# Transposing only the four quarters of a layer's normed rows, and forming the three sums of them afterwards

## The chip, the cores and the metric

The kernel runs on one core of one Trainium2 chip. The metric is the device time of one execution in microseconds (us). Before the change the median of three runs is 982.19 us (982.18 to 983.54). The core has a matrix engine (PE, with its weight loads PEld), a vector engine (DVE), a scalar engine (ACT), GpSimd (POOL) and the queue of SyncE (SP), which only starts transfers here. Each engine works through its own instructions in the order in which they were written; engines meet at semaphores.

## The reference, cut to what matters

```python
def reference(x, mem, norm_g, ...):
    for i in range(2):
        h = rmsnorm(x, norm_g[i])              # (512, 1024)
        mem_h = rmsnorm(mem, mem_norm_g[i])
        proj = jnp.einsum('bsd,de->bse', h, w_in[i])
...
        # layer 0: dilated-window attention, layer 1: grouped-query attention
        o_mem = memory_attention(q_mem, mem_h, ...)
        y = jnp.concatenate([o_mix, o_mem], axis=-1) * jax.nn.silu(gate)
        x = x + jnp.einsum('bse,ed->bsd', y, w_out[i])
    return x
```

The change concerns the step between `h = rmsnorm(...)` and the einsum with the input weights, once in each of the two layers.

## The kernel before, in words

**Products by Strassen's scheme.** The product of the normed rows `h` (512 tokens by 1024 features) with a block of weights is not made as eight products of quarters but as seven, in Winograd's form. For this `h` is cut into quarters: 11 and 12 are the feature halves of the first 256 tokens, 21 and 22 those of the other 256. Seven left operands are needed: 12, 11, S1 = 21 - 22, S2 = S1 - 11, S4 = 12 + S2, S3 = 11 - 21, and 22. They are used in this order (`PRODUCTS`, L350), and a product starts only when its operand is there.

**Two-part numbers.** Each operand goes into the PE as a high and a low part: ACT casts it (the high part, L157), DVE subtracts the high part from it (the low part, L160); both are in the helper `split`. The three matmuls of L163 to L165 make one product of two such pairs. The weights go the same way: a tile `wl` of 128x1024 comes by DMA, ACT casts it to `wh` (L285), DVE subtracts to get `wo` (L295). Sums of weight quarters are made by DVE (L251, L259) at the start and later by accumulating DMAs on the POOL queue. Below, "a weight's low part" is one instruction of L295.

**From rows to operands.** The rows lie with tokens on the partitions, in four blocks of 128 tokens (`xb[0..3]` in layer 0, `x1`, tiles `acc`, in layer 1). A PE matmul needs the features on the partitions, so every operand must be transposed. `norm_1` gets the sums of squares (ACT L451) and POOL the inverse root; `norm_2` scales the rows in place (DVE L458). `turn4` makes four 128x128 transposes on PE (L464) of one 128x512 piece into one PSUM bank `xT`, and `split` takes it out. `put_h` does that for one operand and one token block c. `sum_h` and `sums_h` make the three sums and S1 from the untransposed rows (DVE L499, L507 to L509), and `rest_h` then transposes S2, S4, S3 and 22. So there are 7 operands x 2 blocks x 4 = 56 transposes in a layer, in 14 groups.

**What sets the order.** Nothing is scheduled by a compiler: the Python code is the order on each engine. After each group of matmuls a `Driver` (one "slot") lets waiting generators take one step: those that take products out of PSUM, the weight stream (`W.advance`), and `prep` (layer 0) or `ev_o` (layer 1), which make the operands. The waits between engines are put in by the layer below, which also keeps two engines from using one PSUM bank at a time.

**Layer 0's start** is bare: x and the first weights arrive, and `norm`, transposes, splits and the weight sums follow each other with little else to do. The first product chunk is `s_chunk(512, H, ev_v0, pre=second)`; `second` puts the operands 12 and 11, `prep` the others. **Layer 1's operands** are made in `ev_o` under the end of layer 0's output projection and under `mem_kv(1, ...)`, the projection of the memory rows (matmuls with `act`, heads' transposes `qT`).

Of the kernel before, what the change touches and what calls it, by code (L numbers as in the profile page):

```python
# [11 lines left out]
F32R = mybir.dt.float32r  # L12
AF = mybir.ActivationFunctionType
ALU = mybir.AluOpType
# [12 lines left out]
MEM_STEP = 1, 1  # L27
MEM_D = 4
PD, W_EARLY = 1, True
EO = 1, 2, 1, 1, 1  # L30
YB = {"m": (2, 2), "k": (1, 1, 1), 0: (1, 2, 1), 1: (1, 2, 1)}
Y = [3, 2, 2, 2, 3, 2, 2, 1, 1, 1]

# [91 lines left out]
def trunk_kernel(ctx: ExitStack, tc: tile.TileContext, x, mem, wall, norm_g, mem_norm_g, gcol,  # L125
                 qn_a, kn_a, qn_b, kn_b, ident_d, mask_d, tab_a, tab_b, out):
    nc = tc.nc
    V, A, G, T = nc.vector, nc.scalar, nc.gpsimd, nc.tensor
# [8 lines left out]
    def big(dt=F32, name="big"):  # L137
        return pool.tile([128, 2048], dt, tag="big", name=name, bufs=NBIG)

    def m4(dt=F32, name="m4"):  # L140
        return pool.tile([128, 1024], dt, tag="m4", name=name, bufs=NM4)

    def s2(dt=F32, name="s2"):
        return pool.tile([128, 512], dt, tag="s2", name=name, bufs=NS2)
# [4 lines left out]
    def at(name="at"):  # L149
        return psum.tile([128, 512], F32, tag="at", name=name, bufs=4)  # L150
# [4 lines left out]
    def split(hi, lo, src, act=True):  # L155
        if act:
            A.copy(hi, src)  # L157
        else:
            V.tensor_copy(hi, src)
        V.tensor_tensor(lo, src, hi.bitcast(F32), ALU.subtract)  # L160
# [282 lines left out]
    def norm_1(xb, both=False):  # L443

        ss = sm(2, "ss")
        for j in range(2):
            jk = s2(name="sq")
            if both and j:
                V.tensor_tensor_reduce(jk, xb[j], xb[j], 1.0 / 1024.0, 0.0, ALU.mult, ALU.add, ss[:, j:j + 1])
            else:  # L450
                A.activation(jk, xb[j], AF.Square, scale=1.0 / 32.0, accum_out=ss[:, j:j + 1])  # L451
        r, e = sm(1, "rstd"), sm(1, "mse")
        G.tensor_tensor(e, ss[:, 0:1], ss[:, 1:2], ALU.add)
        return rstd_of(e, 1)

    def norm_2(xb, r, row, js=(0, 1)):
        for j in js:
            V.scalar_tensor_tensor(xb[j], xb[j], r, row[j], ALU.mult, ALU.mult)  # L458

    def turn4(src, hi, lo, mid=None):  # L460

        p = at("xT")
        for k in range(4):
            T.transpose(p[:, k * 128:(k + 1) * 128], src[:, k * 128:(k + 1) * 128], ident)  # L464
        if mid:
            mid()
        split(hi, lo, p.rearrange("p (k t) -> p k t", k=4))

    def norm_3(xb, dst, c0, j):
        cs = slice(c0, c0 + 128)  # L470
        turn4(xb[j], dst.block(0, j, cs), dst.block(1, j, cs))
# [11 lines left out]
                mm3(p, sels[b](act, 0, kk), sels[b](act, 1, kk), w[k][0], w[k][1], kk == 0, kk == 7)  # L483
        chunk(2, len(sels), group, evac)

    part = {}

    def put_h(H, k, c, src, mid=None, early=False):

        if c == 0:  # L490
            part[k] = big(F32R, "h" + k).rearrange("p (a k t) -> p a k t", a=2, k=4)
        if c or early:
            H[k] = part[k]
        cs = slice(c * 128, (c + 1) * 128)
        turn4(src, part[k][:, 0, :, cs], part[k][:, 1, :, cs], mid)

    def sum_h(low):
        s1 = s2(name="xs1")
        V.tensor_tensor(s1, low[0], low[1], ALU.subtract)  # L499
        return s1  # L500

    def sums_h(H, top, low, c, s1, sums):

        (a11, a12), a21 = top, low[0]
        s2_, s4 = s2(name="xs2"), s2(name="xs4")
        put_h(H, "S1", c, s1)
        V.tensor_tensor(s2_, s1, a11, ALU.subtract)  # L507
        V.tensor_tensor(a21, a11, a21, ALU.subtract)
        V.tensor_tensor(s4, a12, s2_, ALU.add)  # L509
        sums.append((s2_, s4, a21, low[1]))  # L510

    def rest_h(H, sums, d=1):
        for i, k in enumerate(("S2", "S4", "S3", "22")):
            for c in range(2):
                put_h(H, k, c, sums[c][i])
            yield d

    def head_sq(p, n=4):
        ss = sm(n, "hss")
# [21 lines left out]
    def halves(t):  # L541
        return [t[:, 0:512], t[:, 512:1024]]
# [7 lines left out]
    def row_bank(name, times=1):  # L550

        r = [at("row") for _ in range(2)]
        for j in (1, 0):
            for _ in range(times):
                T.matmul(r[j], ones, rows[name][j][0:1, :], start=True, stop=True)
        return r
# [282 lines left out]
    H, H2 = {}, {}  # L839
    xb = [halves(t) for t in xt]  # L840
    nst = {}

    def prep():

        s1, sums = [], []
        for c in range(2):
            norm_2(xb[2 + c], nst[2 + c], first)
            s1.append(sum_h(xb[2 + c]))
            yield 1
        for c in range(2):  # L850
            sums_h(H, xb[c], xb[2 + c], c, s1[c], sums)
            yield 1
        yield from rest_h(H, sums)

    def setup():

# [11 lines left out]
    first = row_bank("x0", WARM)  # L868
# [10 lines left out]
    def mid():  # L879
        busy(128)  # L880
        W.lo()
        nst[1] = norm_1(xb[1], BOTH)

    put_h(H, "12", 0, xb[0][1], mid, True)
    if W_EARLY:
        W.hi(True)
# [4 lines left out]
    def second():  # L891
# [9 lines left out]
        nst[3] = norm_1(xb[3], BOTH)  # L901

    drv.spawn(prep(), PD)
    drv.spawn(setup(), SET_AT)

# [264 lines left out]
    x1d = dram.tile([4, 128, D], F32, name="x1d", bufs=1)  # L1170
    row_load("x1", norm_g[1:2, :])

    x1b, sums_b = {}, []

    def ev_o(n, b, x1):
        if n:
            for j in range(2):
                nc.sync.dma_start(x1d[b][:, j * 512:(j + 1) * 512], x1[j])
            r = norm_1(x1)
            yield EO[0]  # L1180
            norm_2(x1, r, rows["x1"])
            x1b[b] = x1
            yield EO[1]
            if b < 2:
                put_h(H2, "12", b, x1[1])
                put_h(H2, "11", b, x1[0])
            else:
                s1 = sum_h(x1)
                yield EO[2]
                sums_h(H2, x1b[b - 2], x1, b - 2, s1, sums_b)  # L1190
            if b == 3:
                yield EO[3]
                yield from rest_h(H2, sums_b, EO[4])

    drv.spawn(mem_norm(1), MEM_B)
    out_proj(YW, ys, xv, ev_o, lambda: [m4(name="acc") for _ in range(2)])


# [302 lines left out]
```

## Time and profile before

| | |
|---|---|
| median of three runs | 982.19 us |
| the profiled execution: time, span | 981.91 us, 980.1 us |
| busy on POOL | 332.2 us (34%) |
| transposes of L464 in the trace | 48 of sums (`xs`), 64 of rows (`x`, `acc`), 32 of memory rows (`m`) |
| moved by DMA | 205.08 MB, mean 209 GB/s |

The span is the time from the first to the last instruction; it lies 1.8 us under the profiled execution's own time. PE does the matmuls and the transposes. A row of the chain of waits names, in order of time, the work that the end hung on, with its start, its length as the chain counts it (up to where the next piece could begin) and its line. A row of the timeline has the start, the busy time, engine, line and operation of one run of equal instructions. A row of the waits has who waited, for whom, how long in total, how often, and the longest.

### The profile page before, as it was taken

The page shows a single profiled execution, that of the slowest core. Times are in us where ns is not written, and L with a number is a line of the kernel's source. Part 1 is how long each engine was busy: PE and PEld are TensorE (multiplying, and loading weights), DVE is VectorE, ACT ScalarE, POOL GpSimd, SP SyncE. Part 2 cuts the span into 40 slices and gives each one's busy share as a digit, 9 for nine tenths or more (in the row PEclk, how much of TensorE's full clock was granted, in tenths as well). Part 3 has the DMA queues.
Part 4 walks back from the last instruction along what each step waited for, and adds up shares of the span by engine and source line. Part 5 has one row for each costly group of instructions (what it writes and reads, how often), then busy time and mean ns, then how long its engine had stood idle before and what let it go on. Part 6 is the DMA issues. An engine that isn't in the chain of part 4 may idle for free.

```text
span 980.1 us, 16658 instructions
## 1 busy us (share of the span) xinstructions
PE 953.1 (97%) x5728; PEld 839.5 (86%) x5728; DVE 825.1 (84%) x1489; ACT 645.7 (66%) x1623; POOL 332.2 (34%) x468
## 2 busy tenths in 40 slices
PE   8899999999999999999999989998999999998998
PEld 5789888888888888888899977887999999997786
DVE  6997788878888888888888998968789998889974
ACT  5556678686767676768676656455677766667650
POOL 1121424556555555555544010124533331011000
PEclk9999999999999999999999999999999999999999
DMA  8979846969686868686949795669695786786432
GB/s 328 329 267 322 227 97 183 290 129 266 152 253 154 251 157 248 158 249 136 271 124 295 228 251 158 258 224 329 168 209 140 189 220 165 230 207 148 144 129 86
DMA packets 86678, 205.08 MB, mean 209 GB/s; under 512 B 25025, under 2 KB 35777, under 8 KB 86594
## 3 DMA queue, kind: packets, MB, share of 16 engines
q1 hardware_dynamic: 70034, 146.28, 42.7%
q0 software_dynamic: 15264, 55.58, 30.1%
q10 hardware_dynamic: 1296, 2.16, 0.6%
q8 instruction: 45, 0.74, 0.3%
q14 instruction: 39, 0.32, 0.1%
HBM read 157.79 MB, written 12.65 MB: 174 GB/s over the span
## 4 chain that ended last, share of the span: by engine, by line
PE 75%; DVE 16%; DMA 3%; issue 2%; ACT 2%; POOL 1%; SPq 0%; DVEq 0%; POOLq 0%
PE pj L163 20%; PE pj L165 19%; PE pj L164 19%; DVE wo L295 4%; PE qT L534 2%; PE oo L1131 1%; PE sa L1029 1%; PE pt L1110 1%; PE sa L1025 1%; PE xT L464 1%; DMA od<-o 1%; DVE sn L370 1%; PE ptb L1333 1%; DVE nmb L1314 1%; DVE yS L763 1%
## 5 line engine op out<-in xcount | busy, mean ns | idle before, releaser
L295 DVE TENSOR_TENSOR wo<-wl,wh 128x1024 fp32r<-128x1024 f32 x255 | 315.5, 1242 | 8.4 <-ACT wh L285 8.0
L285 ACT CAST wh<-wl 128x1024 fp32r<-128x1024 f32 x255 | 269.9, 1059 | 74.1 <-PE pj L165 39.8
L163 PE MATMUL pj<-wh,hS 128*128 128x512 f32 (+1 forms) x448 | 164.3, 367 | 0.2 <-ACT sn L360 0.2
L164 PE MATMUL pj<-wo,hS 128*128 128x512 f32 (+1 forms) x448 | 158.1, 353 | 2.6 <-DVE wo L295 2.6
L165 PE MATMUL pj<-wh,hS 128*128 128x512 f32 (+1 forms) x448 | 158.1, 353 | 0.0
L163 PE MATMUL pj<-wh,h 128*128 128x512 f32 (+1 forms) x336 | 123.2, 367 | 0.0
L164 PE MATMUL pj<-wo,h 128*128 128x512 f32 (+1 forms) x336 | 118.8, 353 | 1.9 <-DVE wo L295 1.9
L165 PE MATMUL pj<-wh,h 128*128 128x512 f32 (+1 forms) x336 | 118.9, 354 | 0.0
L413 POOL TENSOR_TENSOR rstd<-mse,half 128x4 f32<-128x4 f32 (+2 forms) x98 | 103.4, 1055 | 8.2
L164 PEld LDWEIGHTS pj<-wo,hS 128*128 128x128 f32 x448 | 85.0, 190 | 13.4 <-DVE wo L295 3.5
L165 PEld LDWEIGHTS pj<-wh,hS 128*128 128x128 f32 x448 | 84.7, 189 | 12.4 <-DVE hS L160 0.3
L163 PEld LDWEIGHTS pj<-wh,hS 128*128 128x128 f32 x448 | 84.8, 189 | 10.3 <-ACT sn L360 0.4
L360 ACT COPY sn<-pj 128x512 f32<-128x512 f32 x132 | 73.6, 591 | 17.5 <-PE pj L165 17.1
L412 POOL TENSOR_SCALAR mse<-hss 128x4 f32<-128x4 f32 (+1 forms) x86 | 45.7, 532 | 110.2 <-ACT junk L522 103.2
L522 ACT ACTIVATE junk<-sn 128x128 f32<-128x128 f32 x264 | 79.0, 308 | 0.2 <-DVE sn L364 0.2
L973 POOL TENSOR_TENSOR ta<-sn,tabs 128x128 f32<-128x128 f32 (+1 forms) x64 | 37.0, 580 | 120.7 <-DVE sn L527 81.6
L164 PEld LDWEIGHTS pj<-wo,h 128*128 128x128 f32 x336 | 64.0, 191 | 9.5 <-DVE wo L295 2.2
L165 PEld LDWEIGHTS pj<-wh,h 128*128 128x128 f32 x336 | 63.7, 190 | 9.2 <-DVE h L160 0.2
L370 DVE TENSOR_TENSOR sn<-pj,sn 128x512 f32<-128x512 f32 x99 | 67.5, 683 | 4.6 <-PE pj L165 4.4
L163 PEld LDWEIGHTS pj<-wh,h 128*128 128x128 f32 x336 | 63.9, 190 | 7.3 <-ACT h L157 0.2
L269 POOL DMA_DIRECT2D wl<-wl x33 | 29.3, 887 | 114.5 <-DVE wo L295 70.1
L163 PE MATMUL pj<-hS,wh 128*128 128x256 f32 x192 | 55.9, 291 | 0.0
(229 smaller groups left out, 2455.7 us busy)
## 6 DMA issues: line engine op xcount, KB each, us to landing
wl<-in_wall_dram SPq DMA_DIRECT2D x222, 512.0 KB, 6.9
wl<-wl POOLq DMA_DIRECT2D x64, 512.0 KB, 5.8
wl<-in_wall_dram POOLq DMA_DIRECT2D x42, 512.0 KB, 8.3
od<-o SPq DMA_DIRECT2D x12, 256.0 KB, 5.2
og<-od SPq DMA_DIRECT2D x12, 256.0 KB, 5.9
odb<-o SPq DMA_DIRECT2D x12, 256.0 KB, 3.5
og<-odb SPq DMA_DIRECT2D x12, 256.0 KB, 4.6
x<-in_x_dram SPq DMA_DIRECT2D x4, 512.0 KB, 5.7
```

The source lines that it names most:

```text
L163: T.matmul(o, lh, rh, start=start, stop=False, skip_group_check=True)
L164: T.matmul(o, lh, rl, start=False, stop=False, skip_group_check=True)
L165: T.matmul(o, ll, rh, start=False, stop=stop, skip_group_check=True)
L269: G.dma_start(self.tile[key], self.tile[c, "T2", x], accum_op=ALU.add)
L285: A.copy(wh, self.tile[self.items[i]])
L295: V.tensor_tensor(wo, self.tile[key], wh.bitcast(F32), ALU.subtract)
L360: A.copy(t, b)
L370: V.tensor_tensor(t, b, t, ALU.subtract if q == "12" else ALU.add)
L412: G.tensor_scalar(e, ss, EPS, None, ALU.add)
L413: G.tensor_tensor(r, e, half[:, 0:n], ALU.pow)
L522: A.activation(jk, p[:, j * 128:(j + 1) * 128], AF.Square, scale=QS, accum_out=ss[:, j:j + 1])
L973: G.tensor_tensor(ta[:, 0:n], xn[:, 0:n, 0:32], ropeA[:, 0, b, s0:s0 + n], ALU.mult)
```

## The change

Only the four quarters are transposed. `put_h` (used for 12 and 11) also copies the whole transposed piece out of PSUM with ACT into a kept tile `f12` or `f11` of 128x1024. `diffs_h` transposes 22 and 21 of a block, copies 22 into `f22` with ACT, lets DVE form S1 and S3 out of PSUM (21) and the kept tiles, and splits S1. `rest_h` forms S2 and S4 on whole 128x1024 tiles in SBUF and splits S2, S4, S3 and 22 from there, each by one ACT cast and one DVE subtraction of 128x1024. Layer 1's `ev_o` takes one slot less before the S1 of a block.

```diff
-EO = 1, 2, 1, 1, 1
+EO = 1, 2, 1, 1
...
-    def turn4(src, hi, lo, mid=None):
+    def turn(src):
         p = at("xT")
         for k in range(4):
             T.transpose(p[:, k * 128:(k + 1) * 128], src[:, k * 128:(k + 1) * 128], ident)
+        return p.rearrange("p (k t) -> p k t", k=4)
+
+    def turn4(src, hi, lo, mid=None):
+        p = turn(src)
         if mid:
             mid()
-        split(hi, lo, p.rearrange("p (k t) -> p k t", k=4))
+        split(hi, lo, p)
+        return p
...
+    def whole(k, c):
+        if c == 0:
+            full[k] = m4(name="f" + k).rearrange("p (k t) -> p k t", k=4)
+        return full[k][:, :, c * 128:(c + 1) * 128]
+
+    def put_h(H, k, c, src, mid=None, early=False):
+        p = turn4(src, *slot(H, k, c, early), mid)
+        A.copy(whole(k, c), p)
+
+    def diffs_h(H, low, c):
+        f22 = whole("22", c)
+        A.copy(f22, turn(low[1]))
+        p = turn(low[0])
+        s1, s3 = whole("S1", c), whole("S3", c)
+        V.tensor_tensor(s1, p, f22, ALU.subtract)
+        V.tensor_tensor(s3, full["11"][:, :, c * 128:(c + 1) * 128], p, ALU.subtract)
+        split(*slot(H, "S1", c), s1)
+
-    def rest_h(H, sums, d=1):
-        for i, k in enumerate(("S2", "S4", "S3", "22")):
-            for c in range(2):
-                put_h(H, k, c, sums[c][i])
-            yield d
+    def rest_h(H, d=1):
+        def put(k, f):
+            H[k] = big(F32R, "h" + k).rearrange("p (a k t) -> p a k t", a=2, k=4)
+            split(H[k][:, 0], H[k][:, 1], f)
+        s2_, s4 = full["11"], full["12"]
+        V.tensor_tensor(s2_, full["S1"], s2_, ALU.subtract)
+        put("S2", s2_)
+        yield d
+        V.tensor_tensor(s4, s4, s2_, ALU.add)
+        put("S4", s4)
+        yield d
+        put("S3", full["S3"])
+        yield d
+        put("22", full["22"])
+        yield d
...
     def prep():
         for c in range(2):
-            norm_2(xb[2 + c], nst[2 + c], first)
-            s1.append(sum_h(xb[2 + c]))
+            norm_2(xb[2 + c], nst[2 + c], first, (1, 0))
             yield 1
         for c in range(2):
-            sums_h(H, xb[c], xb[2 + c], c, s1[c], sums)
+            diffs_h(H, xb[2 + c], c)
             yield 1
-        yield from rest_h(H, sums)
+        yield from rest_h(H)
...
             else:
-                s1 = sum_h(x1)
+                diffs_h(H2, x1, b - 2)
+            if b == 3:
                 yield EO[2]
-                sums_h(H2, x1b[b - 2], x1, b - 2, s1, sums_b)
-            if b == 3:
-                yield EO[3]
-                yield from rest_h(H2, sums_b, EO[4])
+                yield from rest_h(H2, EO[3])
```

**ACT in layer 0's start.** These are ACT's rows from the second block's operand 12 to the cast of the third weight tile. In square brackets stand the semaphores that an instruction waits for; `xT` is a PSUM bank of transposes, `wl_91` the third weight tile. Before:

```order
L157 CAST h12_134<-xT_172 128x4x128 [waits PE_49]
L157 CAST h11_179<-xT_180 128x4x128 [waits PE_49]
L451 ACTIVATE sq_188,ss_187<-x_80 128x512 [waits DMAHW7_49]
L451 ACTIVATE sq_190,ss_187<-x_80 128x512
L157 CAST h11_179<-xT_200 128x4x128 [waits PE_49]
L285 CAST wh_207<-wl_91 128x1024 [waits DMAHW6_49]
```

and now:

```order
L157 CAST h12_134<-xT_174 128x4x128 [waits PE_49]
L512 COPY f12_157<-xT_174 128x4x128 [waits DVE_49]
L157 CAST h11_182<-xT_183 128x4x128 [waits PE_49]
L512 COPY f11_190<-xT_183 128x4x128 [waits DVE_49]
L451 ACTIVATE sq_193,ss_192<-x_80 128x512 [waits DMAHW7_49]
L451 ACTIVATE sq_195,ss_192<-x_80 128x512
L157 CAST h11_182<-xT_205 128x4x128 [waits PE_49]
L512 COPY f11_190<-xT_205 128x4x128 [waits DVE_49]
L285 CAST wh_213<-wl_91 128x1024 [waits DMAHW6_49]
```

Three copies came between, and each waits for DVE: by its semaphore count, for the subtraction L160 that reads the same bank.

**DVE in layer 0's start.** These are DVE's rows around the operand S2; `wl_101` and `wl_103` are the weight tiles of the products S2. Before:

```order
L160 TENSOR_TENSOR hS2_346<-xT_347,hS2_346 128x4x128 [waits Activation_49]
L160 TENSOR_TENSOR hS2_346<-xT_354,hS2_346 128x4x128 [waits Activation_49]
L370 TENSOR_TENSOR sn_275<-pj_260,sn_275 128x512
L295 TENSOR_TENSOR wo_344<-wl_101,wh_343 128x1024
L160 TENSOR_TENSOR hS4_388<-xT_389,hS4_388 128x4x128 [waits Activation_49]
```

and now:

```order
L530 TENSOR_TENSOR f11_190<-fS1_298,f11_190 128x1024 [waits DVE_49]
L160 TENSOR_TENSOR hS2_358<-f11_190,hS2_358 128x1024 [waits Activation_49]
L370 TENSOR_TENSOR sn_277<-pj_262,sn_277 128x512
L295 TENSOR_TENSOR wo_355<-wl_101,wh_354 128x1024
L533 TENSOR_TENSOR f12_157<-f12_157,f11_190 128x1024
L160 TENSOR_TENSOR hS4_389<-f12_157,hS4_389 128x1024 [waits Activation_49]
L295 TENSOR_TENSOR wo_383<-wl_103,wh_382 128x1024
```

The sum stands right ahead of the subtraction that waits for ACT's cast of that sum, and the weights' low parts stand behind it.

**ACT before layer 1.** These are ACT's rows from the first normed block of layer 1 to the casts of two weight tiles of the memory projection. Before:

```order
L157 CAST h12_7877<-xT_7878 128x4x128 [waits PE_49]
L157 CAST h11_7885<-xT_7886 128x4x128 [waits PE_49]
L451 ACTIVATE sq_7898,ss_7897<-acc_7326 128x512
L451 ACTIVATE sq_7900,ss_7897<-acc_7326 128x512 [waits DVE_49]
L157 CAST h12_7877<-xT_7928 128x4x128 [waits PE_49]
L157 CAST h11_7885<-xT_7935 128x4x128 [waits PE_49]
L285 CAST wh_7956<-wl_7831 128x1024 [waits DMAHW7_49,PE_49,Activation_49]
```

and now:

```order
L512 COPY f12_7850<-xT_7843 128x4x128 [waits DVE_49]
L157 CAST h11_7852<-xT_7853 128x4x128 [waits PE_49]
L512 COPY f11_7860<-xT_7853 128x4x128 [waits DVE_49]
L451 ACTIVATE sq_7867,ss_7866<-acc_7291 128x512
L451 ACTIVATE sq_7869,ss_7866<-acc_7291 128x512
L157 CAST h12_7842<-xT_7897 128x4x128 [waits PE_49]
L512 COPY f12_7850<-xT_7897 128x4x128 [waits DVE_49]
L157 CAST h11_7852<-xT_7905 128x4x128 [waits PE_49]
L512 COPY f11_7860<-xT_7905 128x4x128 [waits DVE_49]
L285 CAST wh_7927<-wl_7796 128x1024 [waits DMAHW7_49,PE_49,Activation_49]
L285 CAST wh_7930<-wl_7798 128x1024 [waits DMAHW0_49,PE_49,Activation_49]
L517 COPY f22_7933<-xT_7934 128x4x128 [waits PE_49]
```

Four copies that wait for DVE stand ahead of the two weight casts, and the copy of 22, which DVE's first difference needs, stands behind the casts.

More of the change, by code (lines that the diff above doesn't have):

```diff
@@ L484, in proj_t, with slot @@
         chunk(2, len(sels), group, evac)
-    part = {}
-    def put_h(H, k, c, src, mid=None, early=False):
+    part, full = {}, {}
+    def slot(H, k, c, early=False):
         if c == 0:
@@ L494, in put_h @@
         cs = slice(c * 128, (c + 1) * 128)
[L495 to L510, printed above, removed]
-    def rest_h(H, sums, d=1):
-        for i, k in enumerate(("S2", "S4", "S3", "22")):
-            for c in range(2):
-                put_h(H, k, c, sums[c][i])
-            yield d
+        return part[k][:, 0, :, cs], part[k][:, 1, :, cs]
+    def whole(k, c):
[28 more added lines that the diff above has]
+        yield d
     def head_sq(p, n=4):
@@ L843, in prep @@
     def prep():
-        s1, sums = [], []
         for c in range(2):
-            norm_2(xb[2 + c], nst[2 + c], first)
-            s1.append(sum_h(xb[2 + c]))
+            norm_2(xb[2 + c], nst[2 + c], first, (1, 0))
             yield 1
         for c in range(2):
-            sums_h(H, xb[c], xb[2 + c], c, s1[c], sums)
+            diffs_h(H, xb[2 + c], c)
             yield 1
-        yield from rest_h(H, sums)
+        yield from rest_h(H)
     def setup():
@@ L1171, in trunk_kernel @@
     row_load("x1", norm_g[1:2, :])
-    x1b, sums_b = {}, []
     def ev_o(n, b, x1):
@@ L1181, in ev_o @@
             norm_2(x1, r, rows["x1"])
-            x1b[b] = x1
             yield EO[1]
```

## The prediction

> **What bounds the kernel now.** First the page: busy shares and the engines of the chain of waits.
>
> ```profile
> PE 953.1 (97%) x5728; PEld 839.5 (86%) x5728; DVE 825.1 (84%) x1489; ACT 645.7 (66%) x1623; POOL 332.2 (34%) x468
> PE 75%; DVE 16%; DMA 3%; issue 2%; ACT 2%; POOL 1%; SPq 0%; DVEq 0%; POOLq 0%
> ```
>
> Over the whole span PE is the bound, so transposes taken off PE look like pure gain. But the change touches two short stretches only, and a share over the span says nothing of them. So next the windows (length; then busy us of PE, PEld, DVE, ACT, POOL; granted clock, DMA share, GB/s) and the waits of these stretches.
>
> ```profile
> 20.00:40.00 20.00, 15.53 (x77) 11.92 (x76) 19.96 (x27) 9.66 (x14) 3.72 (x4) 1.00 0.98 293
> 40.00:60.00 20.00, 20.00 (x106) 16.93 (x105) 16.71 (x22) 14.04 (x27) 2.25 (x6) 1.00 0.66 239
> 665.00:675.00 10.00, 6.67 (x30) 5.30 (x30) 9.09 (x15) 4.89 (x13) 8.46 (x6) 0.86 1.03 354
> PE pj L164 <- DVE wo L295: 4.5, 4, 1.9
> PE xT L464 <- DVE xs L499: 3.3, 2, 1.9
> ```
>
> From 20 to 40 us DVE is busy without a gap and PE only 15.5 of 20 us: in layer 0's start DVE is the bound, and PE waits 4.5 us for weights' low parts. From 40 us on PE is full. Before layer 1 PE stands twice (3.3 us together) for the first difference `xs` (L499), which the change removes. The chain of waits in order of time shows layer 0's start:
>
> ```profile
> 13.53 1.07 ACT h L157 x2
> 14.60 1.23 ACT sq L451 x4
> 15.83 0.48 ACT h L157
> 16.31 0.95 ACT wh L285
> ...
> 18.43 1.41 DVE x L458 x2
> ...
> 26.00 0.60 DVE hS L160
> ...
> 37.74 1.14 DVE wo L295
> ...
> 38.93 0.50 PE pj L164
> ...
> 45.34 0.87 PE xT L464 x8
> 46.21 0.23 PE pj L163
> ```
>
> The end hangs on ACT from 13.5 to 17.3, then on DVE to 38.9, and only then on PE, which issues one 128x512 matmul each 0.23 us. Between 13.5 and 39 us no transpose lies on it. These rows also give the step of each kind, the time until the next can begin: ACT 0.48 for 512 columns, 0.95 for 1024 and 1.23 for a block's squares, DVE 0.60, 1.14, and 0.70 for half a block's norm, a pair of groups of transposes 0.87.
>
> **Layer 0, ACT's part.** The change adds an ACT copy behind each split of 12 and 11, out of the bank that DVE's subtraction L160 reads. By the order with its waits the copy waits for that subtraction. Does such a wait cost? The nearest row is another pair of readers of one bank:
>
> ```profile
> DVE ks L985 <- ACT ks L984: 25.4, 16, 2.3
> L157 ACT CAST h<-xT x12: 583/590/594, 9.1 to 689.7; 128x512 fp32r<-128x512 f32 x12
> L160 DVE TENSOR_TENSOR h<-xT,h x12: 680/684/692, 9.7 to 690.5; 128x512 fp32r<-128x512 f32 x12
> 13.53 1.07 ACT L157 CAST h<-xT 128x512 fp32r<-128x512 f32 x2 [2.92 <-PE xT L464]
> 14.15 1.29 DVE L160 TENSOR_TENSOR h<-xT,h 128x512 fp32r<-128x512 f32 x2 [1.76 <-ACT h L157]
> 17.29 1.23 DVE L295 TENSOR_TENSOR wo<-wl,wh 128x1024 fp32r<-128x1024 f32 x1
> ```
>
> L984 and L985 read different columns of one bank and write different halves of `ks`, and DVE still waits 16 times for ACT (25.4 us). So the wait is real, if that row is read rightly. The Trainium skill ("PSUM — Partial Sum Buffer", section "PSUM bank collisions raise a hardware error") says that ScalarE and VectorE may not use one bank and quadrant at once, two reads included, and that one must guard by bank; this speaks against a second reader, and the row agrees. Without that rule the three copies below would cost 3 x 0.48 = 1.4 us and no waiting.
>
> The price: cast 0.59, hand-over 0.03 (cast at 13.53, subtraction at 14.15), subtraction 0.68, hand-over 0.03, so the copy starts 1.33 us after its cast, and the next ACT instruction 0.48 later. Before, it came 0.48 after the cast. Each `put_h` so holds ACT 1.33 us longer. Of four, the first falls into the 2.92 us for which ACT stood idle before 13.53. The other three, the squares of the third block between them, stand ahead of the cast of the third weight tile. Its low part, which was DVE's at 17.29, comes at 17.29 + 3 x 1.33 = 21.3: **+4.0**. Bounds: +1.4 if the copies waited for nothing, +4.0 if all wait; I take 4.0, since the order holds the waits.
>
> **Layer 0, DVE's part.** From that low part to the one of the first S2 product DVE had no gap. It begins with the last row above; the next rows are its end, the low parts behind it, and the cost of a cast:
>
> ```profile
> L285 ACT CAST wh<-wl 128x1024 fp32r<-128x1024 f32 x255 | 269.9, 1059 | 74.1 <-PE pj L165 39.8
> 37.67 1.21 DVE L295 TENSOR_TENSOR wo<-wl,wh 128x1024 fp32r<-128x1024 f32 x1
> 40.00 2.35 DVE L295 TENSOR_TENSOR wo<-wl,wh 128x1024 fp32r<-128x1024 f32 x2
> ```
>
> In this stretch of 20.38 us the change takes out eight sums (8 x 0.60) and two subtractions for S2 (1.20), 6.0 us. It puts in four differences (2.40), the whole S2 and its subtraction (2.28), a wait of 0.1 for the first cast of S1 and one of about 1.2 for ACT's cast of S2: 1.06 us (L285 has this shape) and hand-overs, with DVE standing, since nothing lies between the sum and its subtraction. Together 6.0: a draw. The other S1 waits are covered by the difference S3 (0.60). So the first S2 weight is ready at 41.8 + 1.2 = 43.0 instead of 38.9, +4.1.
>
> For the second S2 product the low part came at 40.00, 2.33 after the first. Now the sum S4, a wait of 1.2 and the subtraction stand ahead: 1.14 + 1.14 + 1.2 + 1.14 = 4.6, so it starts at 46.4 and ends at 47.6. PE, done with the first at 45.5, stands 2.1 us for it, then needs 11 more steps of 0.23 and is through at 50.1. Before, PE went on to S4 at 46.0 (46.21 as the chain counts), after the transposes at 45.34. From there the casts of S3 and 22 wait for no new sum, DVE leads again (S3's first low part is the sixth step of 1.14 from 46.4, near 53; PE needs it two products' halves of 12 steps after 50.1, at 55.6), and PE is the bound. **Layer 0: 50.1 - 46.0 = +4.1.** The transposes removed are in this (one pair, 0.87, lay at 45.34 where PE is the bound; the earlier ones lay in PE's waits). The delay lasts: PE is full afterwards.
>
> **Layer 1.** The rows (timeline, and PE's around the operands):
>
> ```profile
> 656.13 1.07 ACT L157 CAST h<-xT 128x512 fp32r<-128x512 f32 x2
> 661.04 1.05 ACT L285 CAST wh<-wl 128x1024 fp32r<-128x1024 f32 x1 [0.78 <-ACT h L157]
> 663.10 1.28 DVE L160 TENSOR_TENSOR h<-xT,h 128x512 fp32r<-128x512 f32 x2
> 665.22 4.27 POOL L413 TENSOR_TENSOR rstd<-mse,half 128x4 f32<-128x4 f32 x1
> 672.33 1.09 PE L534 MATMUL qT<-ident,xn 128*128 128x128 f32 x4
> 677.05 1.03 PE L464 MATMUL xT<-ident,xs 128*128 128x128 f32 x8
> ...
> 688.60 1.04 PE L464 MATMUL xT<-ident,acc 128*128 128x128 f32 x8
> 689.39 0.36 PE L163 MATMUL pj<-wh,hS 128*128 128x256 f32 x1
> ```
>
> ACT: two `put_h` from 656.13 on are done 2 x 1.81 later, 659.7, and the squares (1.23) at 661.0, where the next block's cast stands. Its subtraction stands on DVE behind two weights' low parts (663.10); only then come the copy (663.8), cast, subtraction and copy of 11 (to 666.1), and the two weight casts, at 666.1 instead of 661.0. The copy of 22 comes behind them, at 668.0 to 668.6. DVE, done with the last block's norm at 666.9 (two steps of 0.70 from 665.5, the end of the last L160 of 12 and 11), waits for it. Then L520, L521 and the subtraction (1.9), two low parts (2.3), the second block's three (1.9) and the heads' multiply (0.6): 675.4. PE has only the last block's transposes (0.87 from 666.9) and twelve matmuls of 0.23 until 670.5, and then waits for that: `qT` starts at 675.45 instead of 672.33, +3.1. The removed waits for `xs` are replaced by a longer one.
>
> Against this, PE's work from `qT` to the first S1 product took 689.39 - 672.33 = 17.1 us, with four pairs of transposes that are gone (the first and the last are quoted; 4 x 0.87 = 3.5): by PE S1 could start at 689.0, -0.4. But DVE must have its weight's low part: from 675.4 the sum S2 1.1, cast (behind two weight casts on ACT) 1.5, subtraction 1.1, heads 0.6, two low parts 2.3, a block of memory keys 0.7 (put at a norm's step), S4 with its cast 3.4, keys again 0.7, then S3's subtraction, whose cast stands on ACT behind two weight casts (from 685.4: three casts, 3.0), at 688.4 to 689.5, and the low part, 690.7. S1's second matmul (the first to read it) was at 689.6. **Layer 1: +1.1.** The lower bound is -3.5, the transposes alone, if `qT` kept its place and DVE kept up; the upper +3, if POOL's inverse root for the heads takes 4.27 us again and holds the multiply.
>
> **Edits costed at nothing.** The 128x1024 tiles `f` take five buffers of the pool that the weights use, but the row tiles `x` and `acc` go free earlier; in the start the weight loads behind them move by about the same 4 us. If a load came late, it would cost one load less its lead. The added ACT work later in layer 0 (S2's to 22's casts, four of 0.95 instead of eight of 0.48) is level.
>
> **The sum.** 981.91 + 4.1 + 1.1 = 987.1 for the profiled execution; the median lies 0.28 above that, so **987.4**.
>
> **Rivals.**
> *PE's gain shows (faster).* PE is 97% busy, and 12 groups of transposes at 0.44 us go, 5.2 us, with the 3.3 us of stands: 982.2 - 8.5 = 973.7. It needs ACT's copies to be hidden; against it stands the chain, which leaves PE out from 13.5 to 38.9 us. Chance 0.08.
> *The copies wait for nothing.* Then the start costs 1.4 and layer 1 gains some 1: 982.6, no change. The order's waits and the row of `ks` speak against it. 0.06.
> *Layer 1 gains (start as forecast).* If ACT's queue before layer 1 has more air than my walk, PE gives -0.4 to -3.5 there, put at -1.5: 982.2 + 4.1 - 1.5 = 984.8. For it: PE waited there and those waits go. 0.22.
> *Layer 1 loses more.* POOL holds the heads' multiply, and PE, after a stand of 4 us and more, runs at a lower clock, as it did at 0.86 in the window from 665: +3 to +5, 990.3. 0.16.
> *The forecast*, 0.48, its own range 986 to 989.
>
> 0.2% (2 us) is about what a measurement of this kernel tells from no change. Faster by more: 0.08; within: 0.08 (the second rival and the edge of the third); slower: 0.84. The range 984.0 to 991.0 holds the forecast, most of the third and fourth rivals, about 0.8.
>
> **What would show it.** In the changed profile: copies of L512 that wait for DVE L160, three of them between 14 and 21 us; the third weight's low part at 21.3; DVE standing about 1.2 us before L160 of S2 and S4; PE at the S4 product near 50 us; one PE stand of over 4 us near 671 to 675; the first S1 product of layer 1 about 1 us later relative to layer 0's delay. I am wrong if ACT's copies start right behind the casts, or if the low part at 17.3 has not moved: then the start costs nothing and the rivals with a gain hold.

## The result and the profile after

The changed kernel takes 992.09 us (median of six runs, 989.22 to 993.37); before, beside it, 982.45 us (six runs, 981.79 to 983.54). The ratio is 1.0089, 95% interval 1.0078 to 1.0101: 9.6 us slower. The forecast was 987.4 us with a range to 991.0, so the sign was right and the size was not. The profiled execution of the changed kernel took 990.09 us, its span is 988.3 us: 8.2 us over the span before.

First the busy shares on the page of the changed kernel.

```profile
PE 953.3 (96%) x5680; PEld 837.3 (85%) x5680; DVE 824.2 (83%) x1477; ACT 651.1 (66%) x1627; POOL 332.7 (34%) x468
```

PE has 48 transposes fewer and is busy no less (953.1 before). Its mean granted clock is 0.991 against 0.994, which by estimate takes back some 3 us of them (0.003 x 988). ACT is busy 5.4 us longer. None of this says where the time went, so the two traces are compared by the start of one and the same instruction. The next rows are of DVE's timeline, first of the kernel before, then of the changed one, at three marks: the first heads' multiply after layer 0's input, the last low part ahead of layer 1's operands, and a multiply behind them.

```profile
100.55 0.69 DVE L527 TENSOR_TENSOR sn<-sn,rstd 128x512 f32<-128x512 f32 x1 [1.24 <-POOL rstd L413]
639.49 1.29 DVE L160 TENSOR_TENSOR act<-xT,act 128x512 fp32r<-128x512 f32 x2 [1.20 <-ACT act L157]
800.32 0.68 DVE L527 TENSOR_TENSOR sn<-sn,rstd 128x512 f32<-128x512 f32 x1
```

```profile
104.62 0.69 DVE L550 TENSOR_TENSOR sn<-sn,rstd 128x512 f32<-128x512 f32 x1 [1.25 <-POOL rstd L413]
643.10 1.29 DVE L160 TENSOR_TENSOR act<-xT,act 128x512 fp32r<-128x512 f32 x2 [1.68 <-ACT act L157]
808.06 0.69 DVE L550 TENSOR_TENSOR sn<-sn,rstd 128x512 f32<-128x512 f32 x1
```

The shift is 4.07 us at the first mark (104.62 - 100.55), 3.61 at the second and 7.74 at the third. So layer 0's operands cost 4.1 us (forecast 4.1) and layer 1's cost another 4.1 (7.74 - 3.61; forecast 1.1). Between the first two marks 0.5 us is regained, behind the third 0.4 is lost; the spans differ by 8.2.

**Layer 0.** Rows of ACT's and of DVE's timeline in the start of the changed kernel:

```profile
14.82 0.59 ACT L512 COPY f<-xT 128x512 f32<-128x512 f32 x1 [0.76 <-DVE h L160]
16.66 0.59 ACT L512 COPY f<-xT 128x512 f32<-128x512 f32 x1 [0.76 <-DVE h L160]
19.70 0.59 ACT L512 COPY f<-xT 128x512 f32<-128x512 f32 x1 [0.76 <-DVE h L160]
```

```profile
21.27 1.23 DVE L295 TENSOR_TENSOR wo<-wl,wh 128x1024 fp32r<-128x1024 f32 x1 [1.60 <-ACT wh L285]
39.88 1.23 DVE L160 TENSOR_TENSOR hS<-f,hS 128x1024 fp32r<-128x1024 f32 x1 [1.11 <-ACT hS L157]
45.08 1.23 DVE L160 TENSOR_TENSOR hS<-f,hS 128x1024 fp32r<-128x1024 f32 x1 [1.11 <-ACT hS L157]
46.23 1.22 DVE L295 TENSOR_TENSOR wo<-wl,wh 128x1024 fp32r<-128x1024 f32 x1
```

Each copy stands 0.76 us for DVE's subtraction out of the same bank. These three lie between 14 and 21 us (the first of the four, at 10.37, lies ahead), and the third weight's low part comes at 21.27 instead of 17.29. DVE stands 1.11 us before the subtractions of S2 and of S4, since the cast of a whole tile has nothing beside it, and the second S2 weight follows at 46.23.

**Layer 1.** The waits of PE between 640 and 760 us of the changed kernel (for whom, total, times, longest), and rows of ACT and DVE around the first S1 product:

```profile
PE qT L557 <- DVE xn L550: 4.7, 1, 4.7
PE xT L464 <- ACT wh L285: 2.1, 1, 2.1
PE pj L163 <- ACT sn L360: 1.7, 2, 0.9
PE pj L163 <- DVE sn L370: 0.9, 1, 0.9
```

```profile
691.96 1.04 ACT L157 CAST hS<-fS 128x1024 fp32r<-128x1024 f32 x1
692.91 0.58 ACT L623 CAST vm<-pj 128x512 fp32r<-128x512 f32 x1
693.38 1.05 ACT L157 CAST h<-f 128x1024 fp32r<-128x1024 f32 x1
694.33 0.59 ACT L623 CAST vm<-pj 128x512 fp32r<-128x512 f32 x1
694.81 0.60 ACT L360 COPY sn<-pj 128x512 f32<-128x512 f32 x1
...
693.04 1.23 DVE L160 TENSOR_TENSOR hS<-fS,hS 128x1024 fp32r<-128x1024 f32 x1 [1.53 <-ACT hS L157]
694.18 2.35 DVE L295 TENSOR_TENSOR wo<-wl,wh 128x1024 fp32r<-128x1024 f32 x2
696.45 1.22 DVE L160 TENSOR_TENSOR h<-f,h 128x1024 fp32r<-128x1024 f32 x1
697.58 1.28 DVE L625 TENSOR_TENSOR vm<-pj,vm 128x512 fp32r<-128x512 f32 x2
698.78 0.68 DVE L370 TENSOR_TENSOR sn<-pj,sn 128x512 f32<-128x512 f32 x1
```

In the same 120 us PE stood 3.3 us for `xs` before and 0.2 us for an eviction. Now it stands 4.7 us for the heads' multiply, 2.1 for a weight's cast and 2.6 for evictions (`sn`, products taken out of PSUM: L360 on ACT, L370 on DVE). Two of these three stands lie around the first S1 product, 0.85 us at 695.46 and 0.93 at 699.52. The rows show what stands ahead of their evictions, beside pieces of `vm`: the casts and subtractions of the whole tiles S3 and 22, which are used only after the products of S1, S2 and S4. The third, 0.81 us, comes at 727.37 and has another cause. It is read from the chain of waits, first of the kernel before, then of the changed one:

```profile
655.32 6.00 DMA x1d<-acc
...
693.69 7.94 POOL tabs L1211 x4
...
708.41 7.88 DMA wl<-wl
```

```profile
655.19 9.34 DMA x1d<-acc
...
700.82 8.08 POOL tabs L1228 x4
...
715.69 8.34 DMA wl<-wl
```

In both kernels the chain runs through a write of layer 1's rows to DRAM (`x1d`; DVE may scale the rows in place only behind it), and later through four additions on POOL (`tabs`) and a weight's sum made by DMA, which POOL starts behind them. ACT casts this weight and only then takes the product out that PE waits for at 727.37. The cast starts at 724.05 instead of 716.32, 7.7 us later, and that is the shift of the third mark; in all 14 profiles the two shifts agree within 0.03 us.

### The profile page after: what moved, and what is told of

Its sections match the earlier page's. It is cut to its first block, busy times and chain, and to the rows that moved or that the text cites. A ratio compares the mean times of both kernels' runs of the same rounds, so it can differ in the third digit from the quotient of the medians.

```text
span 988.3 us, 16566 instructions
## 1 busy us (share of the span) xinstructions
PE 953.3 (96%) x5680; PEld 837.3 (85%) x5680; DVE 824.2 (83%) x1477; ACT 651.1 (66%) x1627; POOL 332.7 (34%) x468
## 4 chain that ended last, share of the span: by engine, by line
PE 75%; DVE 15%; DMA 3%; ACT 3%; issue 2%; POOL 1%; SPq 0%; DVEq 0%; ACTq 0%; POOLq 0%
PE pj L163 19%; PE pj L165 19%; PE pj L164 19%; DVE wo L295 4%; PE qT L557 2%; PE oo L1152 1%; PE sa L1050 1%; PE pt L1131 1%; PE sa L1046 1%; PE ptb L1350 1%; DMA x1d<-acc 1%; DVE sn L370 1%; DMA wl<-wl 1%; POOL tabs L1228 1%; ACT wh L285 1%
## 5 line engine op out<-in xcount | busy, mean ns | idle before, releaser
L413 POOL TENSOR_TENSOR rstd<-mse,half 128x4 f32<-128x4 f32 (+2 forms) x98 | 101.3, 1034 | 8.2
L360 ACT COPY sn<-pj 128x512 f32<-128x512 f32 x132 | 73.7, 590 | 18.6 <-PE pj L165 18.1
L370 DVE TENSOR_TENSOR sn<-pj,sn 128x512 f32<-128x512 f32 x99 | 67.6, 685 | 5.7 <-PE pj L165 5.5
```

What stands on the lines that cost most here:

```text
L360: A.copy(t, b)
L370: V.tensor_tensor(t, b, t, ALU.subtract if q == "12" else ALU.add)
L413: G.tensor_tensor(r, e, half[:, 0:n], ALU.pow)
```

## The experiments

The shifts below are read at the three marks as above, in the profile of each kernel. "Layer 0" is the shift at the first mark, "layer 1" the shift at the third less that at the second. Times are medians, with the ratio to the kernel before on the same chip (its medians there go from 982.45 to 983.26).

| kernel | time, us | ratio (95%) | layer 0 | layer 1 |
|---|---|---|---|---|
| the change | 992.1 | 1.0089 (1.0078 to 1.0101) | +4.1 | +4.1 |
| layer 0 alone | 988.5 | 1.0054 (1.0039 to 1.0069) | +4.3 | -0.4 |
| layer 1 alone | 986.6 | 1.0037 (1.0024 to 1.0050) | +0.2 | +3.9 |
| copy first | 987.4 | 1.0040 (1.0028 to 1.0052) | +2.4 | +0.7 |
| copies alone, on the kernel before | 987.7 | 1.0046 (1.0028 to 1.0064) | +5.0 | -0.4 |
| busy stand | 992.1 | 1.0087 (1.0059 to 1.0115) | +4.1 | +3.4 |
| sums in halves | 988.5 | 1.0061 (1.0040 to 1.0082) | +2.3 | +2.8 |
| halves, f by POOL | 987.9 | 1.0061 (1.0039 to 1.0082) | +2.4 | +2.7 |
| halves, copy first | 984.6 | 1.0016 (1.0002 to 1.0029) | +0.9 | -0.1 |
| late splits | 991.1 | 1.0089 (1.0066 to 1.0111) | +4.1 | +2.7 |
| layer 1 alone: halves, copy first | 983.3 | 1.0003 (0.9991 to 1.0015) | +0.3 | -1.1 |
| the same, late splits | 981.6 | 0.9989 (0.9976 to 1.0001) | +0.4 | -1.5 |
| halves, copy first, late splits | 984.9 | 1.0018 (1.0004 to 1.0032) | +1.2 | -1.2 |

Where layer 1 is as before, its column still reads -0.4 (in both executions a stretch of half clock is missing that the kernel before has at 672.14), so differences of half a microsecond in these columns say nothing.

**Each layer alone.** In one kernel the old helpers make layer 1's operands, in the other layer 0's (`put_old` is `put_h` as it was).

```diff
-                put_h(H2, "12", b, x1[1])
+                put_old(H2, "12", b, x1[1])
...
-                diffs_h(H2, x1, b - 2)
+                s1 = sum_h(x1)
+                yield EO[2]
+                sums_h(H2, x1b[b - 2], x1, b - 2, s1, sums_b)
```

> Only layer 0 is changed; layer 1 forms and transposes its sums as before. Theory (two separate losses): the start's walk is all there is here: S4's first matmul at 50.1 us and the end some 4 us late, about 986.0 (985.5 to 987). Rival (one loss that grows, for instance a clock that stays lower or loads that stay late): well above 987. Rival (layer 1 holds all of it, the start's delay being regained later): 983 or less.

> Only layer 1 is changed. Theory (the stand before the heads' first transposes and the half clock after it): qT some 4 us and S1's first product 2.5 us later than before, the end 4 to 5 us later, about 986.5. By the forecast's own step (+1.1) it would be 983.5. Rival (layer 1 loses only because it inherits layer 0's delay): 982 or less, since the removed transposes then show.

The costs are two and separate: +5.5 us (988.54 against 983.08) and +3.6 (986.64), together 9.0 of the 9.6. Layer 1 loses as much without layer 0's delay in front, so it doesn't inherit it. Layer 0 alone came out above its expectation, at the number of the rival with loads that stay late, though its walk is the expected one: +4.3 at the first mark. The rest in its profile is one row of DVE's timeline, far from the change,

```profile
545.99 0.69 DVE L783 TENSOR_TENSOR yf<-sn,og 128x512 f32<-128x512 f32 x1 [3.30 <-DMA og<-od]
```

a piece of attention output that is read back from DRAM and landed late (the longest such wait is 0.20 us in the changed kernel, 0.27 with copy first, 1.89 with copies alone, 2.86 in a later run with layer 0 as before). The shift after it is 6.4 instead of 4.4. What sets this landing was not tried. That the two medians add up so nearly is therefore in part luck; by the marks the sum is 4.3 + 3.9 = 8.2.

**Copy first.** ACT copies the transposed piece out of PSUM before the split, and the split reads the copy in SBUF: the same count of instructions, but no second reader of the bank.

```diff
-        p = turn4(src, *slot(H, k, c, early), mid)
-        A.copy(whole(k, c), p)
+        p, f = turn(src), whole(k, c)
+        if mid:
+            mid()
+        A.copy(f, p)
+        split(*slot(H, k, c, early), f)
```

> In both layers ACT first copies the transposed quarter out of PSUM, and the split reads that copy; no second reader of the bank remains, at the same count of instructions. Theory (the copy's wait for DVE's subtraction costs 0.85 us each time beside its own 0.48): the third weight's low part starts at 17.3 + 3 x 0.48 = 18.7 instead of 21.3, layer 0 loses some 1.5 instead of 4.1; layer 1's weight casts come some 3 us earlier; about 987 in all. Rival (DVE's stands before the subtractions of S2 and S4 and the whole-tile casts make the loss): 990 or more, with the start's gain eaten by later waits.

ACT's and DVE's timeline of this kernel:

```profile
14.97 0.58 ACT L514 COPY f<-xT 128x512 f32<-128x512 f32 x1
15.59 0.62 ACT L157 CAST h<-f 128x512 fp32r<-128x512 f32 x1
16.11 0.63 ACT L451 ACTIVATE sq<-x 128x512 f32<-128x512 f32 x1
...
19.55 1.22 DVE L295 TENSOR_TENSOR wo<-wl,wh 128x1024 fp32r<-128x1024 f32 x1 [0.26 <-ACT wh L285]
```

A `put_h` now holds ACT 1.14 us (14.97 to 16.11) instead of 1.82 (13.48 to 15.30), and the low part is at 19.55, 1.7 us earlier than in the changed kernel. That is less than the 2.6 expected, in part because the cast waits for the copy to be written (0.62 from start to start instead of 0.48). The whole kernel came out at the expected 987: 1.7 of layer 0's 4.1 us are gone and 3.4 of layer 1's. The same copies, without a wait for another reader, cost far less.

**The copies alone**, on the kernel before, where nobody reads them.

```diff
+        if k in ("11", "12"):
+            if c == 0:
+                full[k] = m4(name="f" + k).rearrange("p (k t) -> p k t", k=4)
+            A.copy(full[k][:, :, cs], p)
```

> The kernel before, to which only the eight copies of 12 and 11 are added (nobody reads them). Theory: the copies by themselves bring the start's loss, 3 x 1.33 = 4.0 us, since DVE has no gap behind the third weight's low part; layer 1 some 0 to 2; 986 to 988. Rival (the copies lie beside other work; the loss comes from the order of the differences and the casts of whole tiles): 982.4 to 983.5.

They bring layer 0's whole loss by themselves: +5.0 at the first mark, of which 1.0 arose ahead of the first copy (at 11.37 here, 10.37 in the changed kernel), and 4.6 us in the time. In layer 1 they cost nothing. There they hurt only together with the rest of the change, in which DVE stands for the copy of 22 behind them.

**A busy stand.** PE is kept at work ahead of the heads' transposes of layer 1.

```diff
+            if layer and not b:
+                w = at("warm")
+                for i in range(32):
+                    T.transpose(w[:, i % 4 * 128:i % 4 * 128 + 128], ident, ident)
             q = transpose4(xn)
```

> The changed kernel, with 32 transposes of the identity (nobody reads them, 3.5 us at full clock) on PE in the stand ahead of the heads' first transposes of layer 1. Theory (DVE sets S1's start there): the half-clock stretch from 677.8 to 684.7 goes, PE reaches the S1 product some 2 us earlier and then waits there that much longer for evictions and weights' low parts; the time stays within 1 us of the changed kernel's 992.1. Rival (the half clock is what layer 1 lost): about 2 us less, 990.

First the windows of the changed kernel (length; busy us of PE, PEld, DVE, ACT, POOL; granted clock, DMA share, GB/s), then those of this one, a little later:

```profile
674.42:677.83 3.41, 1.09 (x5) 0.56 (x3) 3.33 (x4) 1.56 (x10) 2.14 (x2) 1.00 0.72 250
677.83:681.24 3.41, 1.05 (x5) 1.08 (x6) 3.25 (x5) 3.14 (x11) 2.74 (x4) 0.50 0.94 298
681.24:684.66 3.42, 3.42 (x10) 2.65 (x9) 2.04 (x3) 1.94 (x3) 1.74 (x2) 0.50 0.97 229
```

```profile
692.49:695.91 3.42, 1.68 (x14) 1.48 (x13) 3.42 (x4) 3.42 (x6) 0.00 (x0) 1.00 1.06 280
695.91:699.32 3.41, 3.41 (x18) 3.41 (x17) 3.41 (x5) 0.72 (x1) 0.00 (x0) 0.50 1.02 398
```

The half clock behind the stand is gone, and the time is the same, 992.1. PE began S1 0.7 us earlier (694.79 against 695.46) after a stand of 1.74 us for an eviction, and this second stand brought a stretch of half clock of its own. Layer 1 reads +3.4 instead of +4.1, so the low clock after the first stand, one of the rivals, explains 0.7 at most in this profile.

**Sums in halves.** S2 and S4 are formed and split by halves of 512 columns.

```diff
-        V.tensor_tensor(s2_, full["S1"], s2_, ALU.subtract)
-        put("S2", s2_)
+        put("S2", s2_, full["S1"], s2_, ALU.subtract)
...
+            for cs in cut:
+                V.tensor_tensor(f[:, :, cs], a[:, :, cs], b[:, :, cs], op)
+                A.copy(H[k][:, 0, :, cs], f[:, :, cs])
+            for cs in cut:
+                V.tensor_tensor(H[k][:, 1, :, cs], f[:, :, cs], H[k][:, 0, :, cs].bitcast(F32), ALU.subtract)
```

> The changed kernel, with the sums S2 and S4 formed and split by halves of 512 columns, so that DVE forms the second half while ACT casts the first. Theory (DVE's stands of 1.11 us before the subtractions of S2 and S4 are on the path): they shrink below 0.3, S2's first low part and the second weight come 1 and 2 us earlier, PE is through with S2 near 48.5 instead of 50.1; in layer 1 some 1 us; about 989.5. Rival (the copies hold ACT and set the start alone): 991.5 to 992.5.

DVE's timeline of this kernel:

```profile
37.51 1.29 DVE L531 TENSOR_TENSOR f<-fS,f 128x512 f32<-128x512 f32 x2
38.88 1.30 DVE L534 TENSOR_TENSOR hS<-f,hS 128x512 fp32r<-128x512 f32 x2
...
40.70 1.22 DVE L295 TENSOR_TENSOR wo<-wl,wh 128x1024 fp32r<-128x1024 f32 x1
```

No wait stands before the subtraction any more. S2's weight comes at 40.70 instead of 41.62 and the second one at 44.42 instead of 46.23, as expected; layer 0 loses 2.3 instead of 4.1, layer 1 loses 2.8.

**f by POOL.** As the last run, but POOL adds high and low part of 12 and 11 in SBUF to get `f`, and ACT's eight copies are gone. The sums are kept in a list (`owed`) and issued later, those of layer 0 behind `second`'s other work.

```diff
-        A.copy(whole(k, c), p)
+        f = whole(k, c)
+        owed.append((k, lambda: G.tensor_tensor(f, hi.bitcast(F32), lo.bitcast(F32), ALU.add)))
```

> As the run with halves, but f of 12 and 11 is formed by POOL as the sum of the two parts in SBUF, and ACT's eight copies are gone. Theory (the copies' wait is 4 us of the start and the cause of layer 1's late weight casts): the third weight's low part is back at 17.3, the start costs 0 to 1, layer 1 1 to 2; 983 to 985. Rival (POOL's eight sums of 2 us each slow DVE and hold the heads' inverse roots): 987 or more.

The rival held in the time. POOL's and DVE's timeline of this kernel:

```profile
20.01 6.97 POOL L514 TENSOR_TENSOR f<-h 128x512 f32<-128x512 f32 x4
...
17.61 1.23 DVE L295 TENSOR_TENSOR wo<-wl,wh 128x1024 fp32r<-128x1024 f32 x1 [0.23 <-ACT wh L285]
20.07 2.31 DVE L251 TENSOR_TENSOR wl<-wl 128x1024 f32<-128x1024 f32 x1
23.62 2.21 DVE L295 TENSOR_TENSOR wo<-wl,wh 128x1024 fp32r<-128x1024 f32 x1
25.76 2.30 DVE L251 TENSOR_TENSOR wl<-wl 128x1024 f32<-128x1024 f32 x1
```

ACT's delay is gone (the low part starts at 17.61). But while POOL works, from 20.01 to 26.98, three of DVE's 128x1024 sums take 2.2 to 2.3 us instead of 1.22: 3.2 us given back on the engine that bounds this stretch. The Trainium skill ("GPSIMD Engine Reference", section "1. Specifications") says that GpSimd shares its SBUF interfaces with VectorE and contends with instructions that have two SBUF inputs; these do, and the trace agrees. What keeps layer 1 at +2.7 in this kernel was not settled.

**Copy first and halves together.**

> Copy first and halves together, in both layers. Theory (the two costs add): copy first stood at 987.4, the halves take 2 to 3 off: 984.5 to 985.5. Rival (with the copies out of the way DVE has slack and the halves bring nothing): 987.

984.55 us: the two costs add. Layer 0 keeps +0.9, layer 1 is level.

**Late splits.** In layer 1 the splits of S3 and 22 are put two slots later each.

```diff
-        yield d
+        yield e
         put("S3", full["S3"])
-        yield d
+        yield e
         put("22", full["22"])
...
-                yield from rest_h(H2, EO[3])
+                yield from rest_h(H2, EO[3], 3)
```

> The changed kernel, with the splits of S3 and 22 in layer 1 put two slots of the driver later each, so that they stand behind the evictions of the S1 product on ACT and DVE instead of ahead. Theory (the whole-tile splits hold the evictions, and PE waits for a bank): the waits of 0.85, 0.85 and 0.93 us for `sn` between 694 and 700 go, some 1.5 to 2 us less: 990 to 990.5. Rival (the weights' low parts set this stretch): the waits only change their name, 991.5 to 992.5.

The time, 991.07 (990.81 to 992.22), lies between the two expectations and settles nothing. The profile shows layer 1 at +2.7 instead of +4.1, but most of this 1.4 us is not the splits' work. This execution came into layer 1 already 5.6 us late (2.71 us of waiting for `og` in it), DVE did not wait for the write of `x1d`, and the heads' first transposes came at +3.1 instead of +4.2 (680.98 - 672.33 - 5.58), ahead of any moved split. The evictions do give way: the stands of 0.85 and 0.93 us shrink to 0 and 0.22, and S2's first product comes at +0.7 (698.71 - 692.39 - 5.58) instead of +3.5. But the additions on POOL then take longer,

```profile
700.01 9.01 POOL tabs L1228 x4
```

the weight's sum behind them takes 8.65 us instead of 8.34, and PE stands 0.49 and 1.41 us for later evictions (at 720.04 and 727.90). So the waits mostly change their place, as the rival expected, though not for its reason. (Of the three waits in the theory, one is the 0.81 at 727.37, which no split stands ahead of.) The additions take 9.0 us in all three kernels with late splits. Beside them, here, two of DVE's low parts take 3.46 us instead of 2.36 (at 699.84, against 700.65 in the changed kernel); why was not tried.

The next three kernels put the late splits on versions with copy first and halves:

> Layer 0 as before; layer 1 changed, with copy first and sums in halves. In the run with both in both layers, layer 1 came out 0.2 us better than it went in (+0.6 at 660 us, +0.4 at 720), so theory: level with before, 982.5 to 984. Rival (layer 1 did well only because layer 0's delay had moved its loads): 985 or more.

> As the run before it, with the splits of S3 and 22 two slots later. Theory (the last loss of layer 1 is the evictions behind the splits, 1.5 us): 981 to 982.5, level with before or up to 0.2% faster. Rival: the same time as the run before it.

> Copy first, halves and late splits, in both layers (late in layer 1 alone). Theory: layer 0 keeps its +1.0, layer 1 is level or 1 better: 983 to 984. Rival: 984.5 as without the late splits.

In layer 1 alone the form with halves and copy first is level with the kernel before (983.31 against 983.26). With late splits it takes 981.64, ratio 0.9989, interval 0.9976 to 1.0001; the two intervals overlap, and the profiles differ by 0.5 us: S2's first product comes 1.4 us earlier, but the additions on POOL take 9.0 us instead of 8.1. The waits of PE from 640 to 760 us of that kernel:

```profile
PE qT L590 <- DVE xn L583: 3.1, 1, 3.1
PE pj L163 <- DVE sn L370: 0.7, 2, 0.5
PE pj L163 <- ACT sn L360: 0.7, 1, 0.7
```

Against the changed kernel the stand for the weight's cast is gone, that for the multiply is shorter and the evictions cost 1.4 instead of 2.6. With layer 0 changed as well, late splits brought nothing in the time (984.88 against 984.55, the rival's number), although its profile shows +1.2 and -1.2: the runs spread by 5.5 us there. So no version is faster than before beyond its interval; the best is level, and in its profile layer 1 is 1.5 us ahead.

## Why the prediction was wrong in size

**Layer 0: right, step by step.** The copies wait for L160 (0.76 us, three on the path); the third low part at 21.3, measured 21.27; DVE's stand of 1.2 before S2 and S4, measured 1.11; the second S2 weight from 46.4, measured 46.23; layer 0 in all +4.1, measured +4.07. The steps are shown; that the sum agrees so closely is in part luck, since the first mark reads +0.2 to +0.4 where layer 0 is as before. Copies alone and copy first show that the copies with their wait are enough for it, halves that DVE's stands for the whole-tile casts lie on the path too (1.8 us less without them). Between 100 and 640 us nothing more is lost, so the added ACT work and the larger tiles, costed at nothing, cost nothing there.

**Layer 1: the step that failed is its sum, "+1.1".** Its mechanism held: weights' casts late behind the copies, DVE waiting 1.71 us for the copy of 22, a stand of over 4 us before the heads' transposes, S1 bound by its weight's low part. Three terms were too small, the last one put at nothing. All shifts here are less the 3.6 us of entry.

1. The heads' first transposes: forecast +3.1, measured 680.19 - 672.33 - 3.61 = +4.2. The weight casts came at 670.61, 0.9 later than the walk had them, because DVE's subtraction that the third copy waits for started at 667.57 where the walk had 666.7. DVE was late there since the write of `x1d` held both halves of the next rows until 663.78; before, one half was free at 659.20, which is 1.0 us earlier with the 3.6 of entry. The walk took this write as it was before. DVE's wait for it was 0.90 us here, 0.24 with layer 1 alone and 0 with late splits, and the term goes along: +4.2, +3.6 and +3.1. So the forecast of this term holds where the write is not in the way.
2. The first S1 product: forecast +1.1, measured 695.46 - 689.39 - 3.61 = +2.5. The 1.1 us of the first term ran on through DVE's row: the weight's low part that S1 needs started at 694.18, where the walk had 693.1 (689.5 + 3.6). The rest, 0.3, is the first eviction.
3. What stands behind it: forecast nothing, measured +1.7 (4.1 - 2.5). The walk ended at S1's first product. It followed the whole tiles' casts and subtractions as far as the weights that wait behind them, and not to the evictions that stand in the same queues: S2's first product comes at +3.5 (699.52 - 692.39 - 3.61), 1.1 more than S1's. And it did not follow DVE's delay on to POOL: the additions of `tabs`, which wait for DVE, start 7.1 us later (700.82 - 693.69), the shift of S2's first product, and with 0.1 and 0.5 us more for the additions and for the weight's sum behind them make the 7.7 of the third mark. That part is read from the chain; no run moved the additions or the sum.

The first term does not decide the whole: with layer 1 alone it was 0.7 smaller, and layer 1 lost 3.9 all the same, since the weight's sum behind `tabs` took 8.8 us there. The copies' waits do: with copy first the heads' transposes come at +0.5 (674.80 - 672.33 - 1.93), S2's first product at -0.2 (694.14 - 692.39 - 1.93), and layer 1 loses 0.7, although PE still stands 1.36 and 0.93 us for evictions. The removed transposes then pay for these stands.

The rival "layer 1 loses more" (990.3) was nearer in size, but its reasons are not what the runs show: the low clock cost 0.7 at most (busy stand), and the heads' inverse root on POOL took 1.87 us, not 4.27.

**The median's offset: forecast +0.28, measured +2.0** (992.09 against the profiled 990.09). The changed kernel's six runs spread by 4.2 us, and such an offset is not sure to a microsecond: 29 runs of the kernel before, taken beside the last four experiments, go from 980.33 to 985.99, with a median of 983.26, 1.35 over its profiled 981.91. Things that vary from one execution to the next are in the traces: the landings of `og`, of the write of `x1d` and of the weight's sum (7.9 to 8.8 us), and the place of a stand in the clock's grid (below). How much of the spread each makes was not settled. The runs' mean clocks (0.986 to 0.991) order their times only in part: the slowest, 993.37, has the lowest and the two fastest the highest, but 992.22 has 0.991 too.

Together: 4.1 and 4.1 in the two layers, nothing net elsewhere, and 1.5 by which the median's offset is larger than that of the kernel before in the same comparison (2.00 against 982.45 - 981.91 = 0.54), are the 9.6 measured.

## What to carry to other kernels

Work taken from the fullest engine is worth nothing in a stretch where that engine waits; cost the change there by the queue of the engine that gets the replacement work, and a second reader of a PSUM bank as a wait, not as its own duration. Walk the delay past the first late operand to everything that stands behind the moved instructions in the same queues, evictions above all, and on into the queues that wait for them. If a piece must be both kept and split, copy it out of PSUM first and split the copy, in pieces small enough that one engine works on the next while the other does the last. Splits that nobody needs yet hold the evictions that stand behind them; moving them freed PE here, but most of that was lost again behind POOL, so it is worth a try and no rule.

## What was not expected of the hardware

**PE's clock steps on a grid.** In all traces here the stretches of half clock start and end on a grid of 3.41 us, at another offset in each execution. The two windows of the kernel before that lie around its stand, and two of the kernel with layer 0 alone, read on that grid:

```profile
668.73:672.14 3.41, 1.50 (x9) 0.98 (x7) 3.41 (x6) 2.00 (x3) 3.25 (x4) 1.00 1.03 423
672.14:675.55 3.41, 3.41 (x12) 2.77 (x11) 2.50 (x6) 1.28 (x2) 1.56 (x2) 0.50 1.06 335
```

```profile
675.72:679.13 3.41, 1.50 (x8) 0.95 (x6) 3.41 (x7) 2.40 (x6) 2.94 (x2) 1.00 1.03 419
679.13:682.55 3.42, 3.42 (x19) 2.83 (x20) 2.59 (x5) 1.28 (x2) 1.94 (x2) 1.00 1.06 297
```

PE was busy 1.50 us in both first windows, and the next ran at half clock in the one kernel and at full clock in the other. Counted over the grid stretches at full clock of all 14 profiles, behind the first 10 us: no stretch with less than 1.74 us of standing was followed by half clock, each with more than 1.94 was, and between the two it went either way. So a stand of 2 us may or may not cost a stretch at half speed, by where it falls. The Trainium skill ("TensorE: Matmul & The Clock Gate", section "Part 1: The HAM clock gate") has the free-running window of 3413 ns, which the trace confirms, and gives an idle window as what turns the clock down; here about half a window of standing was enough.

**POOL and DVE.** Additions on POOL nearly doubled the time of DVE's sums from SBUF beside them (2.3 against 1.22 us for 128x1024).
